# The second map's probabilities kept in PSUM, and another place for the modulations' weights, in a two-layer hybrid backbone step

## Chip, cores and metric

One core of one Trainium2 chip. The metric is the device time of one execution in microseconds, as a median over runs. The profile is of one execution of its own, taken by the hardware profiler.

## What is computed

Two layers over 1024 latent tokens and 128 context tokens (1152 in all), width 1024. Each layer modulates a normalised input by a conditioning vector, projects it, mixes it by attention, a Fourier branch and a gated spatial branch, and projects back. The part that matters here is the differential attention of four heads, where each query has two softmax maps, and the modulation:

```
mod = silu(c) @ w_ada + b_ada                  # 1024 x 3072 weights: shift, scale, gate
s = einsum('bhqmd,bhkmd->bhmqk', q, k) * HEAD_DIM**-0.5      # m = 0, 1: two maps
p = softmax(s, axis=-1)
a = p[:, :, 0] - lam * p[:, :, 1]
o = einsum('bhqk,bhke->bhqe', a, v)
o = o * rsqrt(mean(o**2) + RMS_EPS) * subln_w * (1 - lam_init)
```

## The kernel before

Tiles of 128 queries by all 1152 keys. `attention` runs 34 steps a layer: head h = n // 8, query tile i = n % 8. A step n does the following.

- `score(Q, i, 0, zz)` and `score(Q, i, 1, zz)`, one for each map: six matmuls of 384 columns into a tile S of three PSUM banks (line 650), the negated row maximum by VectorE (`nm`, line 652), and the exponential by ScalarE (line 654), which writes the unnormalised probabilities to an SBUF tile P and their sum to `zz`.
- On odd steps from the third on, `values` for a pair of query tiles: 27 matmuls into `pv` (line 674), later a matmul of the squares into the other half of that tile (line 603) and VectorE's reads of it (lines 604, 610).
- `transpose` of the difference of the step before: nine transposes by TensorE into T (line 664), a copy by ScalarE (line 667) and the low part by VectorE (line 668).
- `diff` (`softmax_diff_z1`, lines 591 to 594): reciprocal of the second sum, a factor, and `p1 = p2 * factor + p1` over 128 x 1152 (line 593), whose result the next step transposes.

S, T, pv and the modulations' product `mres` share one PSUM tag of two places, three banks each (`psS`, 6 of the 8 banks); the other two banks hold the tag `mm`. P has a tag of three SBUF places (`tP`), which other stages use for their own tiles. A tile gets its place when an earlier one of its tag is released, that is, when all who read or write it are done. TensorE's order in the attention is that of the code (`manual_schedule`); the other engines' order, and that of the DMA queue on SyncE, is fixed when the program is built, by a list scheduler with priorities. Between a step's parts the generator `fill` gives TensorE projection matmuls of later heads (`mm_dims`, line 387; `mm_tok`, lines 402 and 407), so many ns of them each time (`FILL`, `SHARE`).

The modulations that `start` doesn't make come from the generator `mods(l, part)`: the gate of layer 0, shift and scale of layer 1, and the gate of layer 1. `extra.fill(MFILL)` pulls from it once per part of a step from head 2 on (`MHEAD`), and a pull comes about every 2.2 parts. In a pull, a 128 x 1024 slab of the weights is loaded (line 182) and two sums are advanced by it, one for each of the two conditioning vectors: on VectorE (lines 186, 191), but the second sum of slabs 1, 4 and 7 on ScalarE and GpSimd (lines 188, 189). After eight slabs, a ninth pull loads the bias `ba` (line 161) and adds the sums up by TensorE (`mres`, line 197). The slabs, tag `wr`, share two places with the raw projection weights `wraw` (line 366), the raw output weights, a table and `ba`.

Of the kernel before, what the change touches and what calls it, by code (L numbers as in the profile page):

```python
# [12 lines left out]
AF = mybir.ActivationFunctionType  # L13
# [3 lines left out]
D = 1024  # L17
# [6 lines left out]
CH = 384  # L24
# [24 lines left out]

X_TAGS = {"wr": ("wraw", "woraw", "wada", "tabr", "mr", "ba"), "z": ("zz", "sh", "gt", "vT", "gmt", "gmg", "fot", "vs", "bd", "pqp", "ws", "kc", "vc", "Pp", "modacc"), "Q": ("Q", "bdr", "wsr", "h32"),
          "sq": ("sq", "wft", "dftp", "msq", "bds", "cb")}
X_BUFS = {"wr": 2, "z": 3, "Q": 2, "sq": 3, "X": 2}
X_TAGS = {n: t for t, names in X_TAGS.items() for n in names}

# [6 lines left out]
def backbone_step(ctx, tc, xs, xp, cT, w_ada, b_ada, w_in, w_out, ckT, cv, lamv, wf, wsT, bsT,  # L63
                  ln_g, ln_b, cst, rope, dft, y_s, y_p, new_k, new_v):
    nc = tc.nc
    pe, dve, act, pool, sp = nc.tensor, nc.vector, nc.scalar, nc.gpsimd, nc.sync
# [11 lines left out]
    def psS(shape=(128, 3, 512), name="S"):  # L78
        return ps.tile(list(shape), F32, name=name, tag="S", bufs=2)
# [7 lines left out]
    def tX(shape, name="x", dt=F32):  # L87
        tag = X_TAGS.get(name, "X")
        return wp.tile(list(shape), dt, name=name, tag=tag, bufs=X_BUFS[tag])
# [7 lines left out]
    def tP(shape=(128, TOK), name="p", dt=F32):  # L97
        return bp.tile(list(shape), dt, name=name, tag="P", bufs=3)

# [3 lines left out]
    def small(shape, name, bufs=3, dt=F32):  # L103
        return st.tile(list(shape), dt, name=name, tag=name, bufs=bufs)
# [54 lines left out]
    def mods_bias(l, part):  # L159
        ba = tX([2, D], "ba")  # L160
        sp.dma_start(ba, b_ada[l, part * D:(part + 1) * D].partition_broadcast(2))
        return ba

    def mods_finish(l, part, acc, ba):
        for n in range(2):
            dve.tensor_tensor(ba[:, n * 512:(n + 1) * 512], acc[n], ba[:, n * 512:(n + 1) * 512], op=ALU.add)
        if part == 2:
            sp.dma_start(gate_d[l], ba)
            return
        pt = psM((128, KT, 2), "modt")  # L170
        for kt in range(KT):
            pe.transpose(pt[:, kt, :], ba[:, kt * 128:(kt + 1) * 128], ident[0:2, 0:2])
        if part == 1:
            dve.tensor_scalar(modT[l][:, 1], pt, 1.0, None, op0=ALU.add)
        else:
            dve.tensor_copy(modT[l][:, 0], pt)

    def mods(l, part):
        acc = [tX([128, D], "macc") for _ in range(2)]
        for kt in range(KT):  # L180
            w = tX([128, D], "wada")
            sp.dma_start(w, w_ada[l, kt * 128:(kt + 1) * 128, part * D:(part + 1) * D])
            for c in range(2):
                k = csil[:, kt, c:c + 1]
                if kt == 0:
                    dve.tensor_scalar(acc[c], w, k, None, op0=ALU.mult)
                elif c == 1 and kt in MODS_POOL:
                    act.activation(w, w, AF.Copy, scale=k)
                    pool.tensor_tensor(acc[c], acc[c], w, op=ALU.add)
                else:  # L190
                    dve.scalar_tensor_tensor(acc[c], w, k, acc[c], op0=ALU.mult, op1=ALU.add)  # L191
            yield 1000
        ba = mods_bias(l, part)
        mres = psS((2, 2, 512), "mres")
        for n in range(2):
            for c in range(2):
                pe.matmul(mres[:, n], lhsT=sel2[:, c], rhs=acc[c][:, n * 512:(n + 1) * 512], start=c == 0, stop=c == 1)
        mods_finish(l, part, [mres[:, n] for n in range(2)], ba)
        yield 1000
# [381 lines left out]
    def softmax_diff(l, p1, p2, zz, name):  # L581

        rz = small([128, 2], "rz")
        dve.reciprocal(rz, zz)
        pool.tensor_scalar(p2, p2, rz[:, 1:2], neglam[:, l:l + 1], op0=ALU.mult, op1=ALU.mult)
        return dve.scalar_tensor_tensor(p1, p1, rz[:, 0:1], p2, op0=ALU.mult, op1=ALU.add)
# [32 lines left out]
    class Head:  # L619
# [24 lines left out]
        def score(self, Q, i, m, zz):  # L644
            S, K = psS(), self.K
            ql = slice((i % 2) * 128, (i % 2) * 128 + 128)

            for e, q in enumerate((Q[:, m, ql], qlo[i % 2][:, m])):
                for n in range(3):
                    pe.matmul(S[:, n, :CH], lhsT=q, rhs=K[:, m, n * CH:(n + 1) * CH], start=e == 0, stop=e == 1)  # L650
            nm = small([128, 1], "nm", 4)
            dve.tensor_reduce(nm, S[:, :, :CH], axis=AX.XY, op=ALU.max, negate=True)  # L652
            P = tP(name="P")
            act.activation(P.rearrange("p (c k) -> p c k", c=3), S[:, :, :CH], AF.Exp, bias=nm,  # L654
                           accum_out=zz[:, m:m + 1])
            return P

        def transpose(self, i, a):
# [30 lines left out]
        def prompt(self):  # L689
# [3 lines left out]
            zz = small([128, 2], "zzp", 2)  # L693
            P = tX([128, 2, 128], "Pp")
            for m in range(2):
                S = psM((128, 128), "sp")
                pe.matmul(S, lhsT=self.qp[:, m], rhs=self.kp, start=True, stop=True)
                dve.tensor_reduce(nm[:, m:m + 1], S, axis=AX.X, op=ALU.max, negate=True)
                act.activation(P[:, m], S, AF.Exp, bias=nm[:, m:m + 1], accum_out=zz[:, m:m + 1])  # L699
                yield 0.5 * PACE  # L700
            softmax_diff(l, P[:, 0], P[:, 1], zz, "p")
            yield 0.5 * PACE
# [11 lines left out]
    def attention(l, fill):  # L714

        hd = Qn = None
        turn = None
        done = None
        side = Stream()
        for n in range(8 * H + 2):  # L720
            h, i = min(n // 8, H - 1), n % 8
            if n < 8 * H:
                if i == 0:
                    fill.until((l, U_K + h), (l, U_Q + h), (l, U_V + h))
                    hd = Head(l, h)
                    Qn = hd.pack(0)
                    hd.low(0, Qn)
                if i % 2 == 0:
                    Q = Qn
                if i % 2 == 0:  # L730

                    sums = small([128, 3, 2], "zz2", 4)
                zz = sums[:, i % 2]
                with tc.high_priority(offset=EARLY):
                    p1 = hd.score(Q, i, 0, zz)
                if i < 7:
                    hd.low(i + 1, Qn)
                with tc.high_priority(offset=EARLY):
                    side.fill(1)
                yield h, 0  # L740
                with tc.high_priority(offset=EARLY):
                    p2 = hd.score(Q, i, 1, zz)
                if i % 2 == 0 and i < 6:
                    Qn = hd.pack(i // 2 + 1)
                with tc.high_priority(offset=EARLY):
                    side.fill(1)
                yield h, 1
            if done:
                if done[1] == 0:
                    fill.until((l, U_G + done[0].h))  # L750
                    done[0].begin_values()
                with tc.high_priority(offset=EARLY):
                    finish = done[0].values(done[1])
                with tc.high_priority(offset=EARLY):
                    side.fill(1)
                yield h, 2
                with tc.high_priority(offset=EARLY):
                    finish()
                if done[1] == 0:
                    side.gens.append(done[0].prompt())  # L760
                if done[1] == 3:
                    with tc.high_priority(offset=EARLY):
                        side.drain()
                    done[0].store()
                done = None
            if turn:
                th, ti, ta = turn
                with tc.high_priority(offset=EARLY):
                    th.transpose(ti, ta)
                if ti % 2 == 1:  # L770
                    done = th, ti // 2
                turn = None
                with tc.high_priority(offset=EARLY):
                    side.fill(1)
                yield h, 3
            if n < 8 * H:
                with tc.high_priority(offset=EARLY):
                    hd.diff(i, p1, p2, sums)
                turn = hd, i, p1

    TG = [[0, 1], [2, 3], [4, 5], [6, 7], [8]]

# [393 lines left out]
```

## Time and profile before

| | us |
|---|---|
| Median of 3 runs | 1476.06 (1475.44 to 1478.33) |
| The profiled execution's own time | 1491.39 |
| Its span | 1489.6 |
| TensorE busy | 1352.8 (91%) |
| VectorE busy | 945.2 (63%) |
| ScalarE busy | 732.1 (49%) |
| GpSimd busy | 677.1 (45%) |

Busy shares are means over all stages, and TensorE's busy time rises when its clock falls. What a change in the attention is worth is read there: which instruction of TensorE starts late, and what ended its wait. The first layer's attention takes about 97 to 604 us of the span, the second's about 837 to 1310.

### The profile page before, as it was taken

The page shows a single profiled execution, that of the slowest core. Times are in us where ns is not written, and L with a number is a line of the kernel's source. Part 1 is how long each engine was busy: PE and PEld are TensorE (multiplying, and loading weights), DVE is VectorE, ACT ScalarE, POOL GpSimd, SP SyncE. Part 2 cuts the span into 40 slices and gives each one's busy share as a digit, 9 for nine tenths or more (in the row PEclk, how much of TensorE's full clock was granted, in tenths as well). Part 3 has the DMA queues.
Part 4 walks back from the last instruction along what each step waited for, and adds up shares of the span by engine and source line. Part 5 has one row for each costly group of instructions (what it writes and reads, how often), then busy time and mean ns, then how long its engine had stood idle before and what let it go on. Part 6 is the DMA issues. An engine that isn't in the chain of part 4 may idle for free.

```text
span 1489.6 us, 21465 instructions
## 1 busy us (share of the span) xinstructions
PE 1352.8 (91%) x8264; PEld 1253.0 (84%) x8264; DVE 945.2 (63%) x1514; ACT 732.1 (49%) x1348; POOL 677.1 (45%) x659
## 2 busy tenths in 40 slices
PE   6898998789799799998998999987889999999997
PEld 4698998778589699886888889987878999998786
DVE  3657568677687756346785475777775684535576
ACT  3576566356354245353655665653554543535321
POOL 2454446345342333335687664363462332233652
PEclk9899999899999899999999999999899999999999
DMA  9310111311431322344342111122111121125432
GB/s 339 128 47 20 42 41 49 76 47 38 80 77 35 82 54 65 110 169 147 105 156 71 47 35 30 56 34 77 51 45 24 36 45 36 34 85 191 162 132 88
DMA packets 69470, 118.67 MB, mean 80 GB/s; under 512 B 14188, under 2 KB 45804, under 8 KB 69240
## 3 DMA queue, kind: packets, MB, share of 16 engines
q1 hardware_dynamic: 69368, 117.30, 26.2%
q8 instruction: 65, 1.06, 0.4%
q14 instruction: 37, 0.30, 0.1%
HBM read 99.67 MB, written 17.61 MB: 79 GB/s over the span
## 4 chain that ended last, share of the span: by engine, by line
PE 50%; DVE 18%; DMA 12%; ACT 9%; POOL 4%; issue 4%; SPq 2%; DVEq 0%; POOLq 0%; ACTq 0%
PE z L387 12%; PE y L1035 9%; PE zt L402 8%; PE pv L674 5%; PE S L650 4%; DMA wada<-in_w_ada_dram 4%; PE zt L407 4%; DVE macc L191 2%; ACT P L654 2%; DVE nm L652 2%; DMA kc<-in_ckT_dram 2%; PE T L664 2%; DMA e<-zz 2%; DVE qr L434 2%; DVE P L593 1%
## 5 line engine op out<-in xcount | busy, mean ns | idle before, releaser
L387 PE MATMUL z<-H,w 128*128 128x384 f32 x2520 | 504.3, 347 | 28.0 <-DVE V L507 12.6
L387 PEld LDWEIGHTS z<-H,w 128*128 128x128 f32 x2520 | 448.3, 194 | 35.3 <-DVE V L507 9.7
L654 ACT ACTIVATE P<-S,nm 128x1152 f32<-128x1152 f32 x128 | 156.4, 1222 | 120.0 <-DVE nm L652 110.8
L652 DVE TENSOR_REDUCE nm<-S 128x1 f32<-128x1152 f32 x128 | 172.8, 1350 | 32.9 <-PE S L650 32.9
L402 PE MATMUL zt<-whi,H 128*128 128x256 f32 x1152 | 160.6, 288 | 14.3 <-ACT Pp L699 8.8
L402 PEld LDWEIGHTS zt<-whi,H 128*128 128x128 f32 x1152 | 148.7, 194 | 17.1 <-ACT Pp L699 9.0
L642 POOL TENSOR_TENSOR qlo<-qr,Q 64x128 fp32r<-64x128 f32 x128 | 66.3, 523 | 155.0 <-PE S L650 116.6
L368 POOL TENSOR_TENSOR w<-wraw,w 128x1024 fp32r<-128x1024 f32 x36 | 87.9, 2442 | 93.9 <-ACT w L367 93.2
L650 PE MATMUL S<-K,Q 128*128 128x384 f32 x384 | 96.4, 361 | 30.5 <-DVE a L668 20.4
L674 PE MATMUL pv<-a,V 128*128 128x256 f32 x864 | 112.0, 288 | 5.8 <-ACT P L654 5.8
L674 PEld LDWEIGHTS pv<-a,V 128*128 128x128 f32 x864 | 108.9, 196 | 8.7 <-ACT P L654 8.7
L668 DVE TENSOR_TENSOR a<-T,a 128x1152 fp32r<-128x1152 f32 x64 | 86.6, 1354 | 35.5 <-ACT a L667 35.5
L650 PEld LDWEIGHTS S<-K,Q 128*128 128x128 f32 x384 | 69.4, 199 | 40.7 <-DVE a L668 25.5
L593 DVE SCALAR_TENSOR_TENSOR P<-P,rz 128x1152 f32<-128x1152 f32 x64 | 96.0, 1500 | 1.9
L650 PE MATMUL S<-K,qlo 128*128 128x384 f32 x384 | 92.0, 349 | 0.0
L1035 PE MATMUL y<-wob,mx 128*128 128x512 f32 (+1 forms) x342 | 87.1, 381 | 2.9 <-DVE rr L1037 2.9
L667 ACT ACTIVATE a<-T 128x1152 fp32r<-128x1152 f32 x64 | 72.1, 1126 | 33.2 <-PE T L664 32.9
L191 DVE SCALAR_TENSOR_TENSOR macc<-wada,csil,macc 128x1024 f32<-128x1024 f32 x44 | 62.3, 1438 | 39.2 <-DMA wada<-in_w_ada_dram 39.2
L407 PE MATMUL zt<-wlo,H 128*128 128x256 f32 x576 | 82.8, 284 | 1.4 <-POOL wlo L368 1.4
L1035 PE MATMUL y<-wo,mx 128*128 128x512 f32 (+1 forms) x342 | 82.0, 383 | 0.0
L431 POOL TENSOR_TENSOR sh<-sh,rp 128x384 f32<-128x384 f32 (+1 forms) x48 | 47.2, 984 | 72.6 <-DVE sh L430 72.1
L613 POOL TENSOR_TENSOR msq<-msq,sq 128x256 f32<-128x256 f32 (+1 forms) x40 | 30.2, 756 | 107.6 <-ACT sq L612 100.6
(223 smaller groups left out, 2424.7 us busy)
## 6 DMA issues: line engine op xcount, KB each, us to landing
wraw<-in_w_in_dram SPq DMA_DIRECT2D x52, 512.0 KB, 3.8
wada<-in_w_ada_dram SPq DMA_DIRECT2D x32, 512.0 KB, 3.7
wa<-in_w_ada_dram SPq DMA_DIRECT2D x8, 1024.0 KB, 13.5
woraw<-in_w_out_dram SPq DMA_DIRECT2D x16, 512.0 KB, 3.3
mr<-mix SPq DMA_DIRECT2D x18, 384.0 KB, 3.4
mix<-gs SPq DMA_DIRECT2D x8, 576.0 KB, 3.8
x<-rr SPq DMA_DIRECT2D x9, 512.0 KB, 3.0
xr<-x SPq DMA_DIRECT2D x9, 512.0 KB, 5.6
```

The costliest lines, as they stand in the source:

```text
L191: dve.scalar_tensor_tensor(acc[c], w, k, acc[c], op0=ALU.mult, op1=ALU.add)
L368: eng.tensor_tensor(lo, raw, f(hi), op=ALU.subtract)
L387: pe.matmul(z, lhsT=w[:, a, kt, :], rhs=Hc[c][:, b, kt, :], start=n == 0, stop=n == 23)
L402: pe.matmul(z[:, i, :], lhsT=Hc[c][:, a, kt, o:o + 128], rhs=w[0][:, kt, :], start=n == 0, stop=False)
L407: pe.matmul(z[:, i, :], lhsT=Hc[c][:, 0, kt, o:o + 128], rhs=w[1][:, kt, :], start=False, stop=kt == KT - 1)
L593: dve.scalar_tensor_tensor(p1, p2, c[:, 1:2], p1, op0=ALU.mult, op1=ALU.add)
L650: pe.matmul(S[:, n, :CH], lhsT=q, rhs=K[:, m, n * CH:(n + 1) * CH], start=e == 0, stop=e == 1)
L652: dve.tensor_reduce(nm, S[:, :, :CH], axis=AX.XY, op=ALU.max, negate=True)
L654: act.activation(P.rearrange("p (c k) -> p c k", c=3), S[:, :, :CH], AF.Exp, bias=nm, accum_out=zz[:, m:m + 1])
L668: dve.tensor_tensor(lo, T[:, :, 0:3], f(hi), op=ALU.subtract)
L674: pe.matmul(pv[:, 0, :], lhsT=self.V[:, a, kt, :], rhs=self.A[:, b, kt, :], start=kt == 0 and e == 0, stop=kt == 8 and e == 2)
L1035: pe.matmul(z, lhsT=mx[:, a, k, :], rhs=wo[kt][b][:, ns], start=i == 0, stop=i == 23)
```

## The change

The second map's exponential writes in place, over the scores in PSUM, and `diff` takes its second operand from there; the first map still goes to a P tile in SBUF. The S tile of the second map is so in use until line 593 is done, where before it was free after the exponential. The modulations' slabs leave the tag `wr` and take P places, and the generator yields between a slab's load and its sums, so that the sums stand in the code one pull behind the load. After the eighth slab, its sums and the product `mres` stand in the same pull.

```diff
-X_TAGS = {"wr": ("wraw", "woraw", "wada", "tabr", "mr", "ba"), ...
+X_TAGS = {"wr": ("wraw", "woraw", "tabr", "mr", "ba"), ...
...
         for kt in range(KT):
-            w = tX([128, D], "wada")
+            w = tP((128, D), "wada")
             sp.dma_start(w, w_ada[l, kt * 128:(kt + 1) * 128, part * D:(part + 1) * D])
+            yield 1000
             for c in range(2):
...
                     dve.scalar_tensor_tensor(acc[c], w, k, acc[c], op0=ALU.mult, op1=ALU.add)
-            yield 1000
         ba = mods_bias(l, part)
...
-            P = tP(name="P")
-            act.activation(P.rearrange("p (c k) -> p c k", c=3), S[:, :, :CH], AF.Exp, bias=nm,
-                           accum_out=zz[:, m:m + 1])
+
+            P = tP(name="P").rearrange("p (c k) -> p c k", c=3) if m == 0 else S[:, :, :CH]
+            act.activation(P, S[:, :, :CH], AF.Exp, bias=nm, accum_out=zz[:, m:m + 1])
             return P
...
-                turn = hd, i, p1
+                turn = hd, i, p1.rearrange("p c k -> p (c k)")
```

## Rows read from the trace of the kernel before

**Rows 1.** The page: busy us by engine, its share of the span, instructions.

```profile
PE 1352.8 (91%) x8264; PEld 1253.0 (84%) x8264; DVE 945.2 (63%) x1514; ACT 732.1 (49%) x1348; POOL 677.1 (45%) x659
```

**Rows 2.** The view by windows: stretches of the two attention loops. Columns: stretch, its length, then for PE, PEld, DVE, ACT and POOL the busy us (instructions), the granted share of TensorE's clock, the share of the DMA engines, GB/s. From 338 to 371 us no sums of the modulations run; in the others they do.

```profile
230.00:308.00 78.00, 63.85 (x379) 60.63 (x378) 55.49 (x70) 36.50 (x70) 37.13 (x40) 0.93 0.26 58
308.00:338.00 30.00, 23.14 (x135) 21.77 (x134) 21.88 (x27) 16.67 (x31) 11.84 (x10) 0.94 0.14 44
338.00:371.00 33.00, 30.98 (x192) 29.36 (x192) 25.56 (x38) 21.98 (x43) 21.86 (x26) 1.00 0.15 42
371.00:455.00 84.00, 69.67 (x377) 63.80 (x376) 60.84 (x70) 37.34 (x68) 34.58 (x32) 0.90 0.35 76
...
954.00:1044.00 90.00, 76.64 (x460) 72.76 (x459) 66.72 (x84) 46.07 (x89) 44.67 (x50) 0.96 0.27 68
1044.00:1075.00 31.00, 26.07 (x135) 24.63 (x134) 22.19 (x28) 16.72 (x31) 11.81 (x10) 0.78 0.12 37
```

**Rows 3.** The longest of PE's waits by line over the whole span: whom it waited for: us in total, times, longest us.

```profile
PE S L650 <- DVE a L668: 20.4, 16, 5.5
```

**Rows 4.** The timeline of the first layer's step 8 and the beginning of step 9 (start us, us, engine, line, operation, tiles, shape, count, idle before and what ended it): PE's two score groups of step 9, the difference of step 8, and the evacuation of T.

```profile
200.75 0.16 DVE L591 RECIPROCAL rz<-zz 128x1 f32<-128x1 f32 x1 [1.31 <-ACT P L654]
...
200.91 0.68 PE L650 MATMUL S<-K,Q 128*128 128x384 f32 x3
...
201.20 1.42 DVE L593 SCALAR_TENSOR_TENSOR P<-P,rz 128x1152 f32<-128x1152 f32 x1
...
202.54 1.35 DVE L668 TENSOR_TENSOR a<-T,a 128x1152 fp32r<-128x1152 f32 x1
...
203.94 0.81 PE L650 MATMUL S<-K,Q 128*128 128x384 f32 x3 [0.76 <-DVE a L668]
```

**Rows 5.** The same of the first layer's step 0: DVE's difference, and PE's second score group of step 1.

```profile
106.82 0.79 PE L650 MATMUL S<-K,Q 128*128 128x384 f32 x3
...
108.40 1.49 DVE L593 SCALAR_TENSOR_TENSOR P<-P,rz 128x1152 f32<-128x1152 f32 x1
```

**Rows 6.** The same of the second layer's step 10, the last step before its modulations: PE's two score groups of step 11, and DVE's difference.

```profile
961.98 0.73 PE L650 MATMUL S<-K,Q 128*128 128x384 f32 x3
...
962.35 1.42 DVE L593 SCALAR_TENSOR_TENSOR P<-P,rz 128x1152 f32<-128x1152 f32 x1
...
965.09 0.79 PE L650 MATMUL S<-K,Q 128*128 128x384 f32 x3 [0.28 <-DVE a L668]
```

**Rows 7.** Groups of instructions by line: tiles, shape, count | busy us, mean ns | idle before us and what ended it.

```profile
L654 ACT ACTIVATE P<-S,nm 128x1152 f32<-128x1152 f32 x128 | 156.4, 1222 | 120.0 <-DVE nm L652 110.8 <-DVE zz L594 8.2
...
L593 DVE SCALAR_TENSOR_TENSOR P<-P,rz 128x1152 f32<-128x1152 f32 x64 | 96.0, 1500 | 1.9
...
L668 DVE TENSOR_TENSOR a<-T,a 128x1152 fp32r<-128x1152 f32 x64 | 86.6, 1354 | 35.5 <-ACT a L667 35.5
```

**Rows 8.** The instructions of line 593: least, median and greatest ns, first and last start.

```profile
L593 DVE SCALAR_TENSOR_TENSOR P<-P,rz x64: 1378/1419/3511, 108.4 to 1286.4; 128x1152 f32<-128x1152 f32 x64
```

**Rows 9.** The tile wada: the idle time of engines until its loads had landed (us, times), and its loads' times from issue to landing.

```profile
  DMA wada<-in_w_ada_dram: 44.3, 15
...
DMA to landing us min/median/max: 3.4/3.7/9.6
```

**Rows 10.** The timeline of the first layer's steps 13 and 14: a load, the sums that wait for it, PE behind them.

```profile
261.83 0.33 SPq L182 DMA_DIRECT2D wada<-in_w_ada_dram  x1
...
271.44 2.48 DVE L191 SCALAR_TENSOR_TENSOR macc<-wada,csil,macc 128x1024 f32<-128x1024 f32 x2 [6.36 <-DMA wada<-in_w_ada_dram]
...
275.25 1.33 PE L650 MATMUL S<-K,Q 128*128 128x384 f32 x3 [5.52 <-DVE a L668]
```

**Rows 11.** The timeline of the first layer's step 21: the values of a pair of tiles, the sums of the second modulation, and PE behind them.

```profile
381.74 3.39 PE L674 MATMUL pv<-a,V 128*128 128x256 f32 x27
...
389.96 1.28 DVE L191 SCALAR_TENSOR_TENSOR macc<-wada,csil,macc 128x1024 f32<-128x1024 f32 x1 [8.33 <-DMA wada<-in_w_ada_dram]
...
391.27 1.15 ACT L188 ACTIVATE wada<-wada,csil 128x1024 f32<-128x1024 f32 x1 [8.90 <-DMA msq<-e]
...
392.75 1.22 PE L603 MATMUL pv<-sq,cs 128*128 128x256 f32 x2 [5.72 <-ACT sq L598]
```

**Rows 12.** The timeline of PE around 290 us: an idle stretch, and the values of a pair after it.

```profile
293.19 0.79 PE L387 MATMUL z<-H,w 128*128 128x384 f32 x3 [3.57 <-DVE V L507]
293.82 4.87 PE L674 MATMUL pv<-a,V 128*128 128x256 f32 x27
```

**Rows 13.** The issues of DMAs by line: count, KB of each, median us from issue to landing.

```profile
wada<-in_w_ada_dram SPq DMA_DIRECT2D x32, 512.0 KB, 3.7
...
e<-zz SPq DMA_DIRECT2D x32, 1.0 KB, 8.3
```

**Rows 14.** The timeline of the DMA queue: the first load of the first modulation, and the first of the second one.

```profile
222.14 0.34 SPq L182 DMA_DIRECT2D wada<-in_w_ada_dram  x1
...
344.90 0.34 SPq L182 DMA_DIRECT2D wada<-in_w_ada_dram  x1
```

**Rows 15.** The timeline of POOL: the last sum of the first modulation.

```profile
321.53 2.37 POOL L189 TENSOR_TENSOR macc<-macc,wada 128x1024 f32<-128x1024 f32 x1
```

**Rows 16.** The timeline of PE in the first layer's steps 20 and 21: the transposes T, and the first modulation's product mres.

```profile
367.70 1.14 PE L664 MATMUL T<-cs,P 128*128 128x128 f32 x9
...
373.82 3.60 PE L197 MATMUL mres<-macc,sel 128*2 128x512 f32 x8
```

More of the change, by code (lines that the diff above doesn't have):

```diff
@@ L48 @@
 U_Q, U_K, U_V, U_G, U_F, U_GF, U_U, U_VM, U_GM = 0, 4, 8, 12, 16, 18, 20, 22, 24
-X_TAGS = {"wr": ("wraw", "woraw", "wada", "tabr", "mr", "ba"), "z": ("zz", "sh", "gt", "vT", "gmt", "gmg", "fot", "vs", "bd", "pqp", "ws", "kc", "vc", "Pp", "modacc"), "Q": ("Q", "bdr", "wsr", "h32"),
+X_TAGS = {"wr": ("wraw", "woraw", "tabr", "mr", "ba"), "z": ("zz", "sh", "gt", "vT", "gmt", "gmg", "fot", "vs", "bd", "pqp", "ws", "kc", "vc", "Pp", "modacc"), "Q": ("Q", "bdr", "wsr", "h32"),
           "sq": ("sq", "wft", "dftp", "msq", "bds", "cb")}
```

## The prediction

> **What bounds the kernel.** I read the page first. TensorE is busy 1352.8 us of 1489.6, so a gain has to come out of its idle 137 us, or out of a higher clock [rows 1]. The view by windows then tells where the attention loses time. From 338 to 371 us no sums of the modulations run: TensorE is busy 30.98 of 33 us (6.1% idle), its clock at full grant. In the five stretches with such sums it is busy 63.85 + 23.14 + 69.67 + 76.64 + 26.07 = 259.4 of 313 us [rows 2]. At the quiet share 19.1 us of idle time would lie there; 53.6 do, so the modulations cost 34.5 us of waiting, and the granted share of 0.78 to 0.96 costs more on top: after 3.57 us of idling the 27 matmuls of a pair took 4.87 us, elsewhere 3.39 [rows 11, 12].
>
> The timeline shows the mechanism. VectorE works in a fixed order. At 265 us its next instruction is a modulation sum whose weights were issued at 261.83; it idles 6.36 us, the low part of T queues behind it, and the scores of step 14 wait 5.52 us for the place that T holds [rows 10]. At 390 us the same costs 8.33 us on VectorE, 8.90 on ScalarE behind it, and 5.72 on TensorE [rows 11]. In all, engines idle 44.3 us in 15 waits for these loads [rows 9].
>
> The second thing to read is the two places of tag S. TensorE already waits 20.4 us in 16 waits for the evacuation of T to free one [rows 3].
>
> **Part 1: the second map stays in PSUM.** It removes one SBUF tile per step and moves the release of its S place from the end of the exponential to the end of line 593. On a step without `values` the order of S tiles is: second map of n, T of n-1, first map of n+1, second map of n+1. So the first map of n+1 takes the place of the second map of n, or that of T if it is free earlier. The waiting instruction is a matmul; all of TensorE queues behind it. At step 8 the next scores began at 200.91, and line 593 ended at 201.20 + 1.42 = 202.62: 1.7 us later. The second group of that step then waited 0.8 us for T anyway, which the shift swallows: 0.9 us net [rows 4]. At step 0 it is the second group (106.82) that takes the place, and the difference ends at 109.89: 3.1 us [rows 5]. In the second layer's step 10 it is 963.77 - 961.98 - 0.28 = 1.5 us [rows 6]. I made this subtraction for all 64 steps. In steps 0 to 11 ten places are late, 0.2 to 3.1 us each, the first in rows 5, the last in rows 6: **+13.5 us**. In the odd steps T takes what the finished pair or the difference frees first, and there is slack of 1.5 us or more. In steps 12 to 23, where VectorE is held up by modulation sums, the same subtraction gives 31 us over both layers. These differences are late for a reason that moves, and two of the values (6 us each) are from step 14, which gets no sums any more. Bounds are 0 and 31; I take **+12**, near the ten quiet places.
>
> Line 593 itself reads one operand from PSUM now. The nearest row is line 668, same shape, one operand in PSUM: 1354 ns against a mean of 1500 [rows 7]. That is 64 x 0.146 = 9.3 us of VectorE, of which only the 22 or so places that wait for it count: **-3** (0 to -9). The mean of 1500 comes from a few long ones: the median is 1419, the longest 3511 [rows 8]. The exponential's write to PSUM has no row of its own: no ScalarE instruction writes there. Between 0.1 us faster and slower than its 1222 ns [rows 7], at 22 places, this is -2 to +2; I take 0. The Trainium skill, Perfetto Trace Analysis, section Optimizing Scalar/DVE Operations, puts ScalarE's access at about 51 ns on PSUM and 93 on SBUF; by that, as an estimate, the term would be 22 x 0.042 = -0.9, which no run here shows yet.
>
> The S waits of 20.4 us [rows 3] are of one kind, repeated through the loop. The Trainium skill, Perfetto Trace Analysis, section Optimization Strategy, calls such "consistent bubbles" a sign that there isn't enough SBUF or PSUM for the next tile. By that rule a PSUM tile held longer makes them grow, and nothing that is given back in SBUF helps; the rows bear out the wait, and the growth is what I forecast.
>
> **Part 2: the slabs in P places.** No instruction is added: 32 loads, 52 VectorE and 12 ScalarE and GpSimd instructions as before. What moves is when they can run. Places of a tag are handed out in the order of the code, as I read the queue: the first load runs at 222 us, some 90 us before the code of step 16 that asks for it, because the two `wr` places came free for it; the first load of the second modulation runs at 344.9 [rows 14]. In the new place a slab stands between the P tiles of the steps from 16 on and can't overtake them. The sums of the first modulation so leave steps 10 to 17 for steps 16 to 21, closer to their product. In the kernel before, its last sum ended at 323.90 [rows 15], 50 us ahead of the product at 373.82 [rows 16]. Now the eighth load takes the place that the T of step 20 frees, 367.70 + 1.14 = 368.84; landing 3.7, the sum on VectorE 1.28, ScalarE 1.15, GpSimd 2.37 give 377.3 [rows 11, 13, 15, 16]. The product would be 3.5 us late, more with queues. TensorE stands still meanwhile. The two products of head 3 have longer steps around them and no such wait. Two products of 4 us: **+8** (0 to 20).
>
> The load a step ahead should take VectorE's 44.3 us away. But each sum is still put into VectorE's order at build time right behind the expected landing. What makes loads late are the stores of `e`, 8.3 us to landing each, in the same queue [rows 13]: the load of rows 10 needed over 9 us where 3.7 is the median. These stay, one per two steps. With one place and a half in place of one, I let a third of the modulations' cost go, reckoned on 34.5 us of waiting and some 10 of clock: **-15** (0 to -45). The other gain, `wr` left to the raw weights, is worth little: among TensorE's waits I found none of length for those. On the other hand the first map's exponential can now wait for a P place that a slab holds; at most two P tiles live at once, so the third place is the slab's and a wait is rare: **+2** (0 to 20). SyncE's queue waits for a release as it did.
>
> **Sum:** 13.5 + 12 - 3 + 0 + 8 - 15 + 2 = +17.5 us. The profiled execution, 1491.39 us, would take 1509; it stands 1.04% above the median, and on the median of 1476.06 I forecast **1494 us**.
>
> **Rivals.** (a) *The weights arrive in time, faster.* With the load a whole pull ahead of its sums (about 9 us, longer than nearly every landing), VectorE's waits go nearly all, -40, and with them the lateness of the differences in steps 12 to 23: 13.5 - 3 - 40 + 8 = -21.5: 1455 us. For it speaks that two of the 15 waits alone held TensorE for 5.5 and 5.7 us [rows 10, 11]; against it that the build order, not the code, sets the distance. Chance 0.30. (b) *The hold is covered.* The scheduler knows of the place and puts the difference ahead of other VectorE work; the quiet places shrink to a few us, the loads stay as late as before, and the sum is near zero: 1476. Against it: at step 8 VectorE had idled 1.31 us for the exponential before the reciprocal that line 593 needs, so nothing can be put ahead there [rows 4]. Chance 0.11. (c) *The slabs block the probabilities, much slower.* A P tile that stands behind a slab in the order waits until the slab's sums are done; with a load that lands after 9.6 us and the sums' 2.5 us this passes the 11 us of a step. The exponential, S, and TensorE wait. None of the gain of part 2 gives 17.5 + 15 = +32.5; 1.5 us in each of some 22 steps come to 33 more, and with half of them it is +49: 1525 us. It decides once a load regularly needs more than 8 us. Chance 0.13. The forecast itself, 1480 to 1512, has 0.46.
>
> **Range and chances.** Faster by over 0.2% (about 3 us, what a measurement can tell from no change): 0.30 from (a) and 0.03 from (b), 0.33. Within: 0.08. Slower: 0.46 and 0.13, 0.59. A range from 1452 to 1522 leaves out the far ends of (a) and (c), some 0.15 in all.
>
> **What would show it.** Right: waits of the first map's scores for line 593, one to three us, in steps 0 to 11, where no slab is near; line 593 at about 1.35 us, with no long ones; modulation loads that begin at step 16, not 10, and `mres` waiting for its last sum; VectorE still idle for wada, 25 us or more. Wrong: no wait on line 593 in those steps (b); wada waits under 10 us and the clock at full grant through head 2 (a); ScalarE's exponential idle until a modulation sum (c). The step I trust least is the third that I let go.

## The result, and the profile after

| us | before | after |
|---|---|---|
| Median | 1476.47 (1475.44 to 1478.33, 4 runs) | 1493.05 (1491.75 to 1499.09, 4 runs) |
| The profiled execution's own time | 1491.39 | 1492.21 |
| Its span | 1489.6 | 1490.4 |

Ratio of after to before: 1.0119, 95% interval 1.0089 to 1.0149. The change costs 17 us. The profiled execution of before stood 1% above its timed runs, that of after does not; a second profile of the same kernel before (`e0_before_again`, below: 1469.35 us, span 1467.6) stands beside it where the two differ.

The page of after, its busy line (columns as in [rows 1]):

```profile
PE 1342.3 (90%) x8264; PEld 1246.8 (84%) x8264; DVE 926.2 (62%) x1514; ACT 733.5 (49%) x1348; POOL 653.5 (44%) x659
```

Against [rows 1] VectorE is busy 19 us less and GpSimd 24 us less (14 and 20 against the second profile), and the kernel is slower: it doesn't wait for their total. TensorE's longest waits by line show what it does wait for (answers [rows 3]; the same columns):

```profile
PE S L650 <- DVE P L593: 29.6, 14, 6.6
PE S L650 <- DVE a L668: 12.5, 2, 7.0
...
PE S L650 <- ACT P L655: 6.2, 2, 3.1
...
PE mres L197 <- POOL macc L190: 1.4, 1, 1.4
```

The first line has no counterpart before: 29.6 us of waiting for line 593, while the wait for T's evacuation fell from 20.4 to 12.5 us. Where no slab is near, the places are among those that the prediction named. One thing before traces are laid side by side: the attention does not begin at the same time in each. Its first scores start at 98.80 us in the trace of before, at 96.32 in that of after, and between 96.3 and 100.9 in the experiments below, with or without the change; so only distances within a step are compared. The timeline of the first layer's steps 8 and 9 (answers [rows 4]):

```profile
200.74 0.16 DVE L591 RECIPROCAL rz<-zz 128x1 f32<-128x1 f32 x1 [1.31 <-ACT S L655]
...
201.19 1.42 DVE L593 SCALAR_TENSOR_TENSOR P<-S,rz,P 128x1152 f32<-128x1152 f32 x1
...
202.53 1.35 DVE L668 TENSOR_TENSOR a<-T,a 128x1152 fp32r<-128x1152 f32 x1
...
202.75 0.76 PE L650 MATMUL S<-K,Q 128*128 128x384 f32 x3 [1.69 <-DVE P L593]
...
204.91 0.68 PE L650 MATMUL S<-K,Q 128*128 128x384 f32 x3
```

The difference runs at the same moment as before to 0.01 us, by chance: the trace of after began its attention 2.48 us earlier and has lost about that much by here. It makes the two easy to read together. The next scores begin at 202.75 in place of 200.91, 0.14 us after its end at 202.61, and the second group, which before waited for T until 203.94, begins at 204.91. The step is 0.97 us longer; 0.9 was worked out. Steps 0 and 1 (answers [rows 5]):

```profile
105.92 1.41 DVE L593 SCALAR_TENSOR_TENSOR P<-S,rz,P 128x1152 f32<-128x1152 f32 x1
...
107.40 1.32 PE L650 MATMUL S<-K,Q 128*128 128x384 f32 x3 [3.12 <-ACT P L655]
```

Here it is the second group that stands, 3.12 us, behind a difference that ends at 107.33; 3.1 was worked out. (The times are 2.48 us ahead of those of before: 105.92 here is 108.40 there.) The trace puts that wait down to ScalarE, whose exponential had just ended too. In the kernel before, TensorE waited at the next step's scores instead:

```profile
113.26 0.79 PE L650 MATMUL S<-K,Q 128*128 128x384 f32 x3 [0.45 <-ACT P L654]
...
116.43 0.79 PE L650 MATMUL S<-K,Q 128*128 128x384 f32 x3 [0.82 <-DVE a L668]
```

Both of these waits are gone after the change; the new wait took them in. The view of waits over the first layer's first two heads, 97 to 290 us, gives all of them; over 835 to 1040 us, the second layer's, it has the same two rows with the same numbers:

```profile
PE S L650 <- DVE P L593: 6.3, 4, 2.9
PE S L650 <- ACT P L655: 3.1, 1, 3.1
```

The groups of instructions (answer [rows 7]): busy us, mean ns, idle time before them.

```profile
L593 DVE SCALAR_TENSOR_TENSOR P<-S,rz,P 128x1152 f32<-128x1152 f32 x64 | 90.6, 1415 | 1.9
...
L668 DVE TENSOR_TENSOR a<-T,a 128x1152 fp32r<-128x1152 f32 x64 | 86.6, 1353 | 42.1 <-ACT a L667 41.9
...
L655 ACT ACTIVATE P<-S,nm 128x1152 f32<-128x1152 f32 x64 | 78.3, 1223 | 72.6 <-DVE nm L652 67.1 <-POOL qlo L642 5.2
L655 ACT ACTIVATE S<-S,nm 128x1152 f32<-128x1152 f32 x64 | 76.4, 1193 | 47.7 <-DVE nm L652 42.6 <-DVE zz L594 4.7
```

and line 593 alone (answers [rows 8]): least, median, greatest ns.

```profile
L593 DVE SCALAR_TENSOR_TENSOR P<-S,rz,P x64: 1392/1418/1420, 105.9 to 1288.7; 128x1152 f32<-128x1152 f32 x64
```

The mean of line 593 fell from 1500 to 1415 ns (it is 1469 in the second profile of before), the median only from 1419 to 1418: the long ones went, nothing else. The exponential that writes over its scores takes 1193 ns, the one that writes to SBUF 1223.

The slabs (answers [rows 9]): idle time of engines for the tile wada, and landing.

```profile
  DMA wada<-in_w_ada_dram: 49.4, 11
...
DMA to landing us min/median/max: 3.6/4.1/8.6
```

Idle time for the slabs did not fall. In the second profile of before it was less:

```profile
  DMA wada<-in_w_ada_dram: 41.4, 15
```

The loads run from 292.3 us on, where they began at 222 before. Why they still come late is in two places of the timeline. The first, around 330 us (answers [rows 10]), has a slab's last sums, the next load, and scores that wait:

```profile
328.35 2.68 DVE L192 SCALAR_TENSOR_TENSOR macc<-wada,csil,macc 128x1024 f32<-128x1024 f32 x2 [4.77 <-DMA wada<-in_w_ada_dram]
...
331.05 0.33 SPq L182 DMA_DIRECT2D wada<-in_w_ada_dram  x1
...
334.48 1.33 PE L650 MATMUL S<-K,Q 128*128 128x384 f32 x3 [5.57 <-DVE a L668]
```
The second, around 372 us (answers [rows 11]), has a slab's last sum on GpSimd, the next load, and scores again:

```profile
370.39 2.52 POOL L190 TENSOR_TENSOR macc<-macc,wada 128x1024 f32<-128x1024 f32 x1
...
372.94 0.33 SPq L182 DMA_DIRECT2D wada<-in_w_ada_dram  x1
...
374.53 1.30 PE L650 MATMUL S<-K,Q 128*128 128x384 f32 x3 [6.33 <-DVE P L593]
```

328.35 + 2.68 = 331.03, and the load of the next slab issues at 331.05; 370.39 + 2.52 = 372.91, and the next load issues at 372.94. A slab's load starts when the last sum of the slab before it gives its place back. In both moments one place serves the slabs, and the load that the code puts a pull ahead of its sums has nowhere to go. In all, 18 of the 32 loads issue within 0.05 us of the end of the last sum of the slab before. But so do 16 of the 32 in the kernel before. There the other place of `wr` is not free for slabs either: ten of its loads' waits, 33.6 us, end with line 368, which reads the raw projection weights. SyncE's waits say the same (DMA queue: whom it waited for):

```profile
SPq L677 <- DMA e<-zz: 165.1, 22, 9.3
...
SPq L182 <- POOL macc L190: 43.8, 8, 9.2
```

In the second profile of before the first of these is 134.7 us in 19 waits, the second (there line 189) 22.9 in 6.

### The profile page after: what moved, and what is told of

The parts are those of the page before. It is cut to its first block, busy times and chain, and to the rows that moved or that the text cites. A ratio compares the mean times of both kernels' runs of the same rounds, so it can differ in the third digit from the quotient of the medians.

```text
span 1490.4 us, 21508 instructions
## 1 busy us (share of the span) xinstructions
PE 1342.3 (90%) x8264; PEld 1246.8 (84%) x8264; DVE 926.2 (62%) x1514; ACT 733.5 (49%) x1348; POOL 653.5 (44%) x659
## 4 chain that ended last, share of the span: by engine, by line
PE 43%; DVE 10%; DMA 4%; ACT 4%; POOL 2%; issue 2%; DVEq 0%; SPq 0%; POOLq 0%; ACTq 0%
PE z L387 10%; PE y L1035 10%; PE zt L402 7%; PE S L650 5%; PE pv L674 3%; PE zt L407 3%; DMA wada<-in_w_ada_dram 3%; DVE nm L652 1%; PE T L664 1%; PE dft L945 1%; DVE rr L1052 1%; DVE macc L192 1%; DVE rr L1038 1%; DMA woraw<-in_w_out_dram 1%; DVE bns L205 1%
## 5 line engine op out<-in xcount | busy, mean ns | idle before, releaser
L402 PEld LDWEIGHTS zt<-whi,H 128*128 128x128 f32 x1152 | 149.4, 195 | 13.5 <-ACT ug L789 9.3
L650 PE MATMUL S<-K,Q 128*128 128x384 f32 x384 | 97.2, 364 | 50.6 <-DVE P L593 29.6
L642 POOL TENSOR_TENSOR qlo<-qr,Q 64x128 fp32r<-64x128 f32 x128 | 63.1, 498 | 166.3 <-PE S L650 140.2
L655 ACT ACTIVATE P<-S,nm 128x1152 f32<-128x1152 f32 x64 | 78.3, 1223 | 72.6 <-DVE nm L652 67.1
L655 ACT ACTIVATE S<-S,nm 128x1152 f32<-128x1152 f32 x64 | 76.4, 1193 | 47.7 <-DVE nm L652 42.6
L593 DVE SCALAR_TENSOR_TENSOR P<-S,rz,P 128x1152 f32<-128x1152 f32 x64 | 90.6, 1415 | 1.9
L192 DVE SCALAR_TENSOR_TENSOR macc<-wada,csil,macc 128x1024 f32<-128x1024 f32 x44 | 57.4, 1334 | 49.4 <-DMA wada<-in_w_ada_dram 49.4
```

The lines of the kernel that those rows point to most:

```text
L402: pe.matmul(z[:, i, :], lhsT=Hc[c][:, a, kt, o:o + 128], rhs=w[0][:, kt, :], start=n == 0, stop=False)
L593: dve.scalar_tensor_tensor(p1, p2, c[:, 1:2], p1, op0=ALU.mult, op1=ALU.add)
L655: act.activation(P, S[:, :, :CH], AF.Exp, bias=nm, accum_out=zz[:, m:m + 1])
```

## The experiments

These runs stand on three chips (e0 to e7 on one, e8 to e10 on a second, e11 on a third); the kernel before took 1469 to 1471 us, as a median, on each. Ratios are to the kernel before on the same chip, with 95% intervals.

**The kernel before once more** (`e0_before_again`), no edit.

> The kernel before, unchanged, to see whether its profiled execution of 1491 us is typical. If the profile itself slows a run, this one also takes 1490 us or so with its profile while the runs of before take 1476. If that execution was an odd one, this one takes 1476 us and its trace, not the first, is to be compared with the one after.

Measured: 1469.35 us. What lay above the timed runs was that one execution, not profiling.

**The hold alone** (`e1_hold_alone`): the change without its two edits on the slabs.

```diff
-            P = tP(name="P")
+            P = tP(name="P").rearrange("p (c k) -> p c k", c=3) if m == 0 else S[:, :, :CH]
...
-                turn = hd, i, p1
+                turn = hd, i, p1.rearrange("p c k -> p (c k)")
```

> Part 1 alone: the second map stays in PSUM, the slabs stay in their old places with load and sums in one pull. Theory (the loss is the hold: first scores wait for line 593): ratio 1.015 to 1.020, 1499 to 1506 us, with waits of the scores for line 593 of 25 us or more. Rival (the hold is nearly covered, and the loss is the slabs' move to heads 2 and 3): ratio 1.000 to 1.004.

Measured: 1505.65 us, 1.0228 (1.0188 to 1.0268), above the theory's range. TensorE's waits:

```profile
PE S L650 <- DVE P L593: 33.1, 14, 7.0
```

The hold is the loss, and a larger one than the whole change shows.

**The slabs alone** (`e2_slabs_alone`): both edits on the slabs, the probabilities of both maps in SBUF.

```diff
-            w = tX([128, D], "wada")
+            w = tP((128, D), "wada")
             sp.dma_start(w, w_ada[l, kt * 128:(kt + 1) * 128, part * D:(part + 1) * D])
+            yield 1000
```

> Part 2 alone: slabs in places of P with their load a pull ahead, both maps in SBUF. Theory: ratio 0.99 to 1.00, since the slabs' waits move without growing. Rival: ratio 1.008 to 1.012, the whole loss.

Measured: 1488.98 us, 1.0111 (1.0074 to 1.0147). Slower too; the rival's number for this run, but without the rival's small cost for the hold. TensorE's longest wait:

```profile
PE T L664 <- ACT P L654: 21.5, 5, 7.3
```

and what ScalarE's exponentials waited for, where it was a release and not their own input (the kernel before has neither row):

```profile
ACT P L654 <- PE T L664: 11.2, 4, 5.6
...
ACT P L654 <- DVE macc L192: 10.7, 1, 10.7
```

With two P tiles a step and a slab in three places, an exponential waits for the transposes of an older P tile (11.2 us in four waits), and once for a slab's sum (10.7 us); the transposes behind wait 21.5 us. This is rival (c) of the prediction, in the kernel without the hold. In the changed kernel these rows are gone, and the transposes' wait for an exponential is 1.5 us: the second map needs no P place there.

**The moved yield alone** (`e3_shift_alone`).

```diff
             sp.dma_start(w, w_ada[l, kt * 128:(kt + 1) * 128, part * D:(part + 1) * D])
+            yield 1000
...
-            yield 1000
         ba = mods_bias(l, part)
```

> Only the yield between a slab's load and its sums; slabs in their old places, both maps in SBUF. Theory: within 0.3% of before, since the order that the engines get is made from expected times and not from the pull. Rival (the load ahead hides the landing): ratio 0.985 to 0.995, idle time for wada under 20 us in place of 44.

Measured: 1470.23 us, 0.9994 (0.9975 to 1.0013). Nothing, as the theory had it.

**A late read of the scores** (`e4_late_read`, `e8_late_read_after`): both maps in SBUF, one more small operation of VectorE that reads the score tile of the second map. The first copies a column; the second adds a column of line 593's result to it.

```diff
+                    dve.tensor_copy(small([128, 1], "late", 1), s2[:, 0, 0:1])        # e4
+                    dve.tensor_tensor(small([128, 1], "late", 1), s2[:, 0, 0:1],      # e8
+                                      p1[:, 0:1], op=ALU.add)
```

> Both maps' probabilities stay in SBUF as before; only a copy of one column of the second map's scores by VectorE is added behind line 593, so that the score tile's place is held about as long as in e1_hold_alone, plus some 0.06 us. Theory (the hold of the place is what costs): ratio 1.018 to 1.027, with TensorE's score groups waiting some 25 to 40 us in all for the copy, as they wait 33.1 us for line 593 in e1. Rival (what e1 lost comes from writing the probabilities over the scores and from line 593's operand in PSUM, not from the place): 1.000 to 1.004.

Measured: 1477.03 us, 1.0042 (1.0010 to 1.0075). The upper edge of the rival's range, but it told little: the copy ran ahead of line 593 (104.35 against 105.87 us in step 0 of this trace; the 108.4 in the next expectation is from the trace of before, whose attention began 2.5 us later) and so didn't hold the place as long.

> As e4_late_read, but the added operation of VectorE reads a column of the second map's scores and a column of line 593's result, so that it can't run ahead of line 593, as e4's copy did (it started at 104.3 us where line 593 of that step started at 108.4). The place is so held about 0.15 us longer than in e1_hold_alone, and the probabilities stay in SBUF. Theory (the hold is what costs): ratio 1.019 to 1.030, TensorE's score groups waiting 28 to 45 us for the added operation. Rival (e1's loss comes from writing over the scores or from line 593's operand in PSUM): 1.002 to 1.008.

Measured: 1528.95 us, 1.0402 (1.0368 to 1.0436), over the theory's range and far from the rival's. TensorE's waits:

```profile
PE S L650 <- DVE a L668: 31.1, 12, 4.8
PE S L650 <- DVE late L779: 26.8, 11, 4.3
PE T L664 <- DVE late L779: 15.3, 5, 6.2
```
The added operation's own row (least, median, greatest ns):

```profile
L779 DVE TENSOR_TENSOR late<-S,P x64: 118/148/159, 109.5 to 1324.6; 128x1 f32<-128x1 f32 x64
```

The added operation itself takes 0.15 us, but it ends 1.0 us after line 593 on the mean of 64 (median 0.55, longest 6.3), because VectorE's order puts other work between. The probabilities are in SBUF here and nothing is written in place, so holding the place in PSUM costs by itself. The loss is larger than in e1, and the hold is longer; but the added operation also takes a place in VectorE's order, and how much of the excess comes of the longer hold was not measured.

**Without the later modulations** (`e5_before_no_mods`, `e6_hold_no_mods`): the 32 loads and their 64 partial products left out, the sums set to zero; the second with the hold of e1.

```diff
-            w = tX([128, D], "wada")
-            sp.dma_start(w, w_ada[l, kt * 128:(kt + 1) * 128, part * D:(part + 1) * D])
...
+                    dve.memset(acc[c], 0.0)
```

> Leaves out the later modulations' 32 weight loads and their 64 partial products; their sums are set to zero. Prediction's account: the modulations cost 34.5 us of TensorE's waiting and some 10 us of clock, so this is 35 to 55 us below the kernel before, ratio 0.963 to 0.976. If TensorE's idle time in those steps has another cause: 0.985 to 1.000.

> The second map's probabilities over their scores, in the kernel without the later modulations' loads and sums (left out as in e5_before_no_mods). Read against e5, it is the hold's cost where no modulation delays VectorE. Theory (the hold cost 33 us in e1 because modulation sums delay line 593 while it holds the place): 13 to 25 us above e5, 0.9 to 1.7% of it. Rival (the hold costs as much without them): 28 to 38 us. Second rival (it costs only there): under 6 us.

Measured: 1418.58 us, 0.9645 (0.9591 to 0.9699), and 1436.06 us, 0.9734 (0.9682 to 0.9786). The modulations cost 3.55% of 1470, 52 us. The hold without them costs 0.89%, 13 us by the ratios, 17.5 by the medians, 21.1 by the spans (1435.9 - 1414.8): the lower part of the theory's 13 to 25. The 13 us are good to some 10, so the times alone hardly tell it from the second rival's 6; the waits do. What the score groups waited for in e5 (lines are 8 lower in these two: 585 is 593, 642 is 650, 660 is 668):

```profile
PE S L642 <- DVE a L660: 8.3, 8, 1.8
```
and in e6:

```profile
PE S L642 <- DVE P L585: 25.1, 16, 2.9
```

No modulation sum runs there, and TensorE waits 25.1 us for the difference.

**The change without its moved yield** (`e7_no_shift`).

```diff
             sp.dma_start(w, w_ada[l, kt * 128:(kt + 1) * 128, part * D:(part + 1) * D])
-            yield 1000
...
+            yield 1000
         ba = mods_bias(l, part)
```

> The change without its moved yield: probabilities over their scores and slabs in P places, a slab's load and its sums in the same pull. Theory (the moved yield does nothing, as alone in e3_shift_alone): as the changed kernel, 1.009 to 1.015 of the kernel before. Rival (with the slabs in P places the load a pull ahead is what hides the landing): 1.018 or more, with engines idle for the slabs for well over the 49.4 us of the changed kernel.

Measured: 1488.77 us, 1.0115 (1.0079 to 1.0150), as the changed kernel. Engines idle 44.6 us for the slabs, no longer than in the changed kernel, so the rival's sign is missing too.

**The slabs' loads in ScalarE's queue** (`e9_slabs_on_act_queue` in the changed kernel, `e10_before_act_queue` in the kernel before).

```diff
-            sp.dma_start(w, w_ada[l, kt * 128:(kt + 1) * 128, part * D:(part + 1) * D])
+            act.dma_start(w, w_ada[l, kt * 128:(kt + 1) * 128, part * D:(part + 1) * D])
```

> The changed kernel with the slabs' loads issued by ScalarE's queue in place of SyncE's. In the changed kernel SyncE's queue stands 165.1 us in 22 waits before the read of e (line 677) until e's store has landed, with loads queued behind. Theory (this queue, not the landing, keeps the weights late): engines' idle time for the slabs falls from 49.4 us to under 30, ratio 0.995 to 1.005 of the kernel before. Rival (the place comes free only with GpSimd's sum of the slab before, 43.8 us of SyncE's waits, and now ScalarE stands there instead): idle for the slabs stays over 40, ratio 1.012 to 1.035.

Measured: 1501.38 us, 1.0225 (1.0187 to 1.0264). The theory fell, the rival's signs came:

```profile
  DMA wada<-in_w_ada_dram: 54.3, 16
...
DMA to landing us min/median/max: 3.4/3.6/6.8
```

The landing itself is short (median 3.6, longest 6.8 us), and engines still stand 54.3 us for the slabs: neither the landing nor SyncE's queue is what keeps them late. In 13 of the 32 loads the issue comes within 0.15 us of the last sum of the slab before, which is the place; others stand in ScalarE's order, behind its own instructions.

> The kernel before with the slabs' loads issued by ScalarE's queue. Same question where nothing else is changed. Theory (SyncE's queue keeps the weights late): idle for the slabs falls from some 42 us to under 25, ratio 0.980 to 0.993. Rival (a wait for a place holds ScalarE, and exponentials behind it): 1.003 to 1.025.

Measured: 1467.49 us, 0.9971 (0.9947 to 0.9995). Neither range:

```profile
  DMA wada<-in_w_ada_dram: 30.2, 15
...
DMA to landing us min/median/max: 3.4/3.7/8.9
```

Idle time for the slabs falls from 41.4 to 30.2 us where they share two places with the raw weights, and some 0.3% of the time with it, barely more than its interval. Of the versions that leave nothing out it is the only one whose interval lies below the kernel before.

**More work behind the transposes** (`e11_more_cover`).

```diff
-SHARE = [0.75, 1.25, 1, 1]
+SHARE = [0.5, 1.0, 1, 1.5]
```

> The changed kernel with other shares of filling matmuls in the parts of a step: 1.5 in place of 1 of a part's filling behind the transposes, where the next scores stand waiting for line 593, and 0.25 less behind each score group, so that a step fills as much as before. In the first head that is 0.8 us more between the transposes and the next scores (0.5 of 1600 ns). Theory (the hold leaves a hole of 1 to 3 us behind the transposes that other matmuls can fill): TensorE's waits for line 593 fall from 29.6 us to under 20, and the ratio to the kernel before to 1.000 to 1.008. Rival (VectorE's chain, not TensorE's order, sets the step, and the filling only trades one wait for another): 1.009 to 1.018, with waits on VectorE growing elsewhere.

Measured: 1520.95 us, 1.0343 (1.0318 to 1.0368), slower than either expectation.

```profile
PE S L650 <- DVE msq L610: 20.6, 3, 9.6
PE z L387 <- ACT Pp L699: 19.4, 4, 8.5
PE S L650 <- DVE P L593: 11.9, 7, 3.0
```

The waits for line 593 did fall, from 29.6 to 11.9 us, and others came that are larger. A new share moves every projection and modulation behind it; what of the loss that is was not taken apart. So waits for line 593 can be covered, but these shares lose more than that.

## Why the prediction came out

The forecast was 1494, the median 1493.05, and the ratio gives 17.6 us where the sum was 17.5. That the sum fits does not mean that its terms do. The runs allow the account by parts, in ratios to the kernel before:

| | slabs in `wr` | slabs in P places | no slabs |
|---|---|---|---|
| second map in SBUF | 1 | 1.0111 (e2) | 0.9645 (e5) |
| second map over its scores | 1.0228 (e1) | 1.0119 (the change) | 0.9734 (e6) |

What the modulations cost, as the difference to the last column times 1470 us:

| | slabs in `wr` | slabs in P places |
|---|---|---|
| second map in SBUF | 52 us | 68 us |
| second map over its scores | 73 us | 57 us |

From the intervals each is good to some 8 to 10 us. Read down the last column, the hold costs 13 us by the ratios (13 to 21 by all three measures) where no sum delays VectorE, and the modulations cost 57 us after the change against 52 before, which these runs can't tell from no difference. Read so, the change is the hold, and nothing that shows from the slabs. This is one reading, because the two halves don't add: alone they cost 33.5 and 16 us, together 17.5, and read along the first row the slabs cost 16 us and the hold on top of them 1. What speaks for the hold in the changed kernel is its trace, with 29.6 us of waits for line 593 and without the waits for a P place that the slabs cause in e2.

*The hold.* "+13.5" for ten quiet places: right in kind, too large. In steps 0 to 11 TensorE waits for line 593 at six places, not ten, behind steps 0, 8 and 10 of each layer: 3.12 + 1.69 + 1.59 us, 12.8 over both layers. From that go the waits that the kernel before had and that are gone: 0.76 us behind step 8, which the working took off, and 0.45 + 0.82 us at step 2, which it did not. Some 8.7 us remain, and the times agree: from the first scores of step 0 to those of step 12 the changed kernel takes 143.9 us in the first layer and 142.4 in the second, e2, which has no slab there either, 139.4 and 138.1, together 8.8 us less. Other pairs of traces give 6.5 (e6 less e5) to 9.9 (against e0), as the first head alone takes 92.3 to 94.6 us from trace to trace without the hold.

"+12" for steps 12 to 23, out of 0 to 31: too low for the hold by itself. The hold alone cost 2.28% of 1470, 33.5 us, so some 25 us beside the quiet places; without modulations it costs 13 to 21 in all (e6). That the excess needs the modulations is what e1 and e6 show together. That it comes of sums that delay line 593 is shown for a part: the waits for line 593 are 33.1 us in e1 and 25.1 in e6, the longest 7.0 and 2.9, and in head 1 the hold costs 4.0 us with sums (117.6 us in e1, 113.6 in e0) and 1.9 without (103.9 in the changed kernel, 102.0 in e5). Where the rest of the excess lies was not taken apart. In the changed kernel 29.6 - 2 x 6.3 = 17.0 us of waits for line 593 lie from head 2 on, the two longest of 6.3 and 6.6 us.

*Line 593.* "-3", on 1354 ns: the mechanism failed, the size was small. The nearest row was not near: line 668 is another instruction, and an operand in PSUM left the median at 1418 ns. What VectorE gained, 96.0 - 90.6 = 5.4 us (3.4 from the second profile's 94.0), are the long ones (last section).

*The exponential's write.* "0", between -2 and +2: in place it takes 1193 ns beside 1223, so 22 places are worth -0.7 us. The Trainium skill, Perfetto Trace Analysis, section Optimizing Scalar/DVE Operations, had given -0.9 by 51 against 93 ns; the row shows 30 ns less, not 42.

*The growth of the wait on S.* TensorE's scores wait for VectorE 29.6 + 12.5 us after, where the wait for T's evacuation took 20.4 before [rows 3]. The Trainium skill, Perfetto Trace Analysis, section Optimization Strategy, reads such repeated gaps as a possible sign of too little memory for the next tile, and the trace agrees: of PSUM, not of the SBUF that the change freed.

*The products.* "+8": wrong. `mres` waits 1.4 us for its last sum, once. In the first layer the eighth load issues at 357.89 us, not at 368.84, the last sum ends at 372.91 (worked out: 377.3), and TensorE, held at 374.53 by line 593, comes to the product at 379.07.

*A third of the modulations' cost.* "-15", on "one place and a half in place of one", "the step I trust least": wrong against the kernel before. The idle time for slabs went from 41.4 to 49.4 us, the cost from 52 to 57; no gain shows. The move gave the slabs no more place than they had: 18 of 32 loads start right behind the last sum of the slab before, where 16 did, and the loads' waits for GpSimd's sum make 43.8 us, where they made 22.9. The prediction had put the lateness down to the stores of `e`, in the same queue. In e10 the loads are in another queue, and the longest landing is still 8.9 us. What stands in SyncE's queue is the read of `e` (line 677) that waits for the store, 165.1 us in 22 waits, with loads behind it, and that was so before. In the kernel before a queue of their own brings 0.3% (e10); in the changed one it makes things worse, 1.0225 against 1.0119 (e9).

*The exponential waiting for P.* "+2": about right in the changed kernel, where no such wait shows. Without the hold it is 21.5 us (e2). That is where the change's two halves belong together: each alone makes the modulations 16 to 21 us dearer, and together they don't. Counted after the hold, the slabs' move gives 33.5 - 17.6 = 16 us back, near "-15" but for another reason: it undoes what the hold adds.

So the sign and the kind of wait were right by their reason. That the total came out to 0.1 us is luck: +13.5 was some 5 us too high, +12 too low for the hold by itself, and the two large terms of part 2, +8 and -15, were wrong by their reasons and sum to -7 where nothing was found. Of the rivals, (a) fell with the 49.4 us of idling for slabs, (b) with the waits in steps 0 to 11, and (c) is what the slabs do without the hold. Of the signs named, loads that begin at step 16 and VectorE idle for them over 25 us came; line 593 at 1.35 us didn't, though its long ones went, and `mres` hardly waited.

Open are why e11 lost so much, why the two halves cost so much more alone than together, and what of the clock is in each term: its mean grant is 0.974 in e0, 0.963 in the profile after, 0.958 in e1.

## What to carry to other kernels

A tile written in place saves a place in one memory and lengthens the life of one in the other; the subtraction "when is the next holder ready, and when does the last reader end", made step by step on the trace of before, found the wait at steps 0, 8 and 10. Its sum was too high, 13.5 us for some 9, since waits of before that the new ones take in have to be taken off everywhere, and some were not. A load put earlier in the code comes earlier only if a place is free: look at what ended just before it starts. And two edits that each cost may not add up: e1 and e2 lose 3.4% in sum, both together 1.2%.

## What the hardware showed beside that

GpSimd stretches a VectorE instruction with both operands in SBUF, and not the same instruction with one of them in PSUM. The timeline of e5 in a step where line 593 (585 here) starts together with GpSimd's split of the keys:

```profile
231.48 3.11 POOL L433 TENSOR_TENSOR K<-zz,K 64x384 fp32r<-64x384 f32 x2 [1.69 <-ACT K L432]
231.48 2.23 DVE L585 SCALAR_TENSOR_TENSOR P<-P,rz 128x1152 f32<-128x1152 f32 x1
```
and the same step of e6:

```profile
232.29 1.42 DVE L585 SCALAR_TENSOR_TENSOR P<-S,rz,P 128x1152 f32<-128x1152 f32 x1
232.30 2.10 POOL L433 TENSOR_TENSOR K<-zz,K 64x384 fp32r<-64x384 f32 x2 [1.21 <-ACT K L432]
```

2.23 against 1.42 us, and GpSimd's pair 3.11 against 2.10. Over the whole span the longest in e6 is 1420 ns, in e5 2230. Where VectorE starts first, it is GpSimd that pays. Another step of e5:

```profile
145.12 1.42 DVE L585 SCALAR_TENSOR_TENSOR P<-P,rz 128x1152 f32<-128x1152 f32 x1
145.19 3.30 POOL L433 TENSOR_TENSOR K<-zz,K 64x384 fp32r<-64x384 f32 x2 [0.98 <-ACT K L432]
```
and the same step of e6:

```profile
145.79 1.42 DVE L585 SCALAR_TENSOR_TENSOR P<-S,rz,P 128x1152 f32<-128x1152 f32 x1
145.86 2.06 POOL L433 TENSOR_TENSOR K<-zz,K 64x384 fp32r<-64x384 f32 x2 [0.98 <-ACT K L432]
```

Line 593 takes its 1.42 us in both, and GpSimd's pair takes 1.24 us longer in e5. In e5 line 593 meets a GpSimd instruction 40 times; in 38 of them one of the two takes longer, in two neither does. The Trainium skill, SBUF — State Buffer, section Who interferes with whom, has it that a VectorE instruction with two inputs in SBUF contends with a GpSimd instruction that reads SBUF, and that one with at most one, outside VectorE's two-port modes, doesn't; these rows agree. In this kernel it is worth 0.8 us of VectorE at a few places, less than the hold that came with it; GpSimd is busy 641.9 us in e5 and 622.7 in e6, with 647 instructions in each.
